# Small counting steps placed between the steps of a sort, a product moved from VectorE to ScalarE, and an activation table loaded early

The chip is one Trainium2; the kernel runs on one of its cores. The metric is device time in microseconds (us) of one launch, lower is better.

## The reference

A graph attention layer: 4096 nodes with 64 features, 50000 edges, 4 heads of 64 outputs, all in fp32. Loops over heads are written short here.

```python
x_proj[h] = x @ weight[h]
score[h, e] = sum(x_proj[h, src[e]] * att_src[h]) + sum(x_proj[h, dst[e]] * att_dst[h])
score = where(score > 0, score, 0.2 * score)
output[h, dst[e]] += exp(score[h, e]) * x_proj[h, src[e]]
total[h, dst[e]]  += exp(score[h, e])
return (output / (total + 1e-8)).transpose(1, 0, 2).reshape(4096, 256)
```

The edges come in random order. The kernel sorts them twice on VectorE, so that all edges of a block of destinations lie together, and then works block by block.

## The kernel before

The edges lie as 128 rows of 391. A first sort orders each row and merges rows in runs of eight. It is a chain of compare steps, each a pair of VectorE instructions (a minimum and a maximum) that read one buffer and write the next. The sorted rows are stored to memory, and for each group of nodes the right stretch of every run is fetched back. Where a stretch starts follows from counting how many sources lie below a bound. That takes three engines: ScalarE forms a Sign against each of sixteen bounds and adds it up (`below`), TensorE adds the rows of a run (`counts`), and VectorE turns that into addresses (`bounds`).

```python
def runs(self, to=None, fine=0, between=()):
    ...
    for m in range(1, 3):                      # the second and third round of merging rows
        self.turn()                            # transpose
        self.opposed(m)
        for j in range(m - 1, -1, -1):
            self.half(j)
        self.turn()
        last = fine if m == 2 else 0
        todo = list(between) if m == 2 else []
        for j in range(8, last - 1, -1):
            self.half(j, to=to if m == 2 and j == last else None)
            if todo:
                todo.pop(0)(self.a[self.cur])  # one small step behind each pair
...
def bounds(pool, cps, nt, n, off, mask, nk, ws, we):
    for i, ps in enumerate(cps):               # two counts, seven small instructions each
        cnt = pool.tile([P, nt + 1], F32, name=f"cnt{i}")
        V.tensor_scalar(out=cnt[:], in0=ps[:], scalar1=-0.5, scalar2=RUN * n / 2, ...)
        for o, t in ((0, ws), (1, we)):
            ...                                # pick, reduce, add the offset
...
def fetch(pool, skey, start, n, to, what):
    if start.dtype == I32:
        wi = start
    else:
        wi = pool.tile([P, w], I32, name=f"wi{what}")[:]
        V.tensor_copy(out=wi, in_=start)       # the addresses as integers
    for i in range(w):
        G.indirect_dma_start(out=to[:, i * n:(i + 1) * n], in_=skey[:, :], in_offset=..., ...)
...
sgn = below(so1, av(eS[:], 0, [2, EL]), EL, nb1, NR, NR)
for e, n in ((0, EH), (EH, EL - EH)):          # the sort keys, in two halves
    V.tensor_scalar(out=sli[:, c], in0=src, scalar1=SG - 1, ..., op0=OP.bitwise_and)
    V.tensor_scalar(out=tF[:, c], in0=sli[:, c], scalar1=1.0 - N, ..., op0=OP.mult)
    V.scalar_tensor_tensor(out=uF[:, c], in0=dst, scalar=float(SG), in1=tF[:, c], ...)
    V.scalar_tensor_tensor(out=key[:, c], in0=src, scalar=float(N), in1=uF[:, c], ...)
tables(pr, pps, pp1)                           # attention tables: TensorE and ScalarE
so.rows(1, EL)
cps = counts(so1, pp1, sgn, NR, [sel1[:, 0, :], sel1[:, 1, :]])
store(skey1, so.runs())
bounds(so1, cps, NR, EL, off1, m16, NR, ws1, we1)
...
stretches = group(so2, Lent(), ws1[:], (relative, split))   # fetch, then the second sort
```

In the traces each engine takes its instructions in the order of the program. `tables` stands ahead of `counts`, and both use TensorE.

## Time and profile before

| | us |
|---|---|
| median of 3 runs (range) | 292.44 (291.14 to 292.70) |
| span of the profiled run | 291.7 |
| VectorE / TensorE / ScalarE busy | 262.4 / 202.9 / 185.7 |
| first step of the first sort | 6.88 |
| counts on TensorE | 62.66 |
| sorted rows stored, stretches fetched | 68.18, 72.39 |
| first step of the second sort | 76.55 |

The prediction below shows the seam between the sorts and the lines around it. What it only refers to is the start. These are lines of the timeline of the kernel before; the columns are start in us, busy us, engine, line of the source, operation, output and inputs with shapes, number of instructions, and in brackets the idle time in front with what ended it.

```profile
4.38 0.26 DVE L697 TENSOR_SCALAR tF<-sli 128x195 f32<-128x195 int32 x1
4.68 0.36 DVE L698 SCALAR_TENSOR_TENSOR uF<-eD,tF 128x195 f32<-128x195 int32 x1
...
5.48 1.28 ACT L279 ACT_TABLE_LOAD   x1 [5.48 <-DVE key L699]
...
6.77 0.65 ACT L279 ACTIVATE junk<-eS,nb 128x391 f32<-128x391 int32 x1
6.88 0.36 DVE L200 TENSOR_TENSOR sA<-key 128x196 f32<-128x196 f32 x1
```

The key is made on VectorE, line by line. ScalarE loads its table (1.28 us) only at 5.48, because in the program as built the load carries the first Sign's waits for the edges; the bracket names VectorE, which ended at the same moment.

### The profile page before, as it was taken

The numbers are of one execution on the slowest core, as the hardware profiler recorded it, in microseconds if no ns is written. First come the engines' busy times: TensorE is split into PE (matmuls) and PEld (weight loads), VectorE is DVE, ScalarE is ACT, GpSimd is POOL, SyncE is SP. The second block draws the span as 40 slices with busy tenths as digits, with TensorE's granted clock in tenths as the row PEclk, the third lists the DMA queues.
The fourth block names the chain that finished last, engine by engine and source line by source line (L and its number), as shares of the span: only waits on it lengthen the run. The fifth ranks groups of instructions, "written<-read, shape, count | busy, mean of one in ns | idle before, by whom it ended". The sixth has DMA issues, their size and how long they took to land.

```text
span 291.7 us, 8543 instructions
## 1 busy us (share of the span) xinstructions
PE 202.9 (70%) x3546; PEld 194.6 (67%) x3546; DVE 262.4 (90%) x536; ACT 185.7 (64%) x360; POOL 27.6 (9%) x78
## 2 busy tenths in 40 slices
PE   0001899970000027478999999999999999999990
PEld 0000599970000015268999999999999999999980
DVE  5999999996499999698999999999999999999970
ACT  2960710031499946484787878888888878787850
POOL 7882000000200000600000000000000000000000
PEclk9999975555555558887999999999999999999998
DMA  3026000001100001186776767767586757675011
GB/s 110 0 50 115 0 2 0 0 1 37 36 0 0 0 0 39 50 322 212 274 292 218 280 234 256 252 237 285 204 286 229 287 199 299 234 265 183 22 37 42
DMA packets 13327, 40.75 MB, mean 140 GB/s; under 512 B 3121, under 2 KB 8913, under 8 KB 9313
## 3 DMA queue, kind: packets, MB, share of 16 engines
q1 hardware_dynamic: 10768, 37.91, 36.2%
q10 hardware_dynamic: 1808, 1.56, 2.4%
q0 software_dynamic: 704, 0.66, 0.9%
q8 instruction: 30, 0.49, 0.7%
q14 instruction: 17, 0.13, 0.1%
HBM read 35.08 MB, written 5.05 MB: 138 GB/s over the span
## 4 chain that ended last, share of the span: by engine, by line

## 5 line engine op out<-in xcount | busy, mean ns | idle before, releaser
L531 ACT CAST xs<-ps 128x1200 bf16<-128x1200 f32 (+1 forms) x99 | 103.9, 1049 | 0.0
L549 DVE TENSOR_TENSOR val<-xs,wv 128x4096 bf16<-128x4096 bf16 (+1 forms) x34 | 75.4, 2221 | 0.4 <-ACT xs L531 0.2
L523 PE MATMUL ps<-adb,oh 128*128 128x136 bf16 x528 | 62.1, 224 | 0.0
L574 PE MATMUL acc<-xs,val 128*128 128x125 bf16 x1024 | 61.8, 218 | 0.0
L521 PE MATMUL ps<-xa,oh 128*128 128x72 bf16 x528 | 59.4, 197 | 3.4 <-DVE oh L500 2.2
L574 PEld LDWEIGHTS <-val 128*128 128x128 bf16 x1056 | 58.8, 98 | 0.0
L523 PEld LDWEIGHTS <-oh 128*128 128x128 bf16 x528 | 49.5, 99 | 1.3 <-issue 1.2
L521 PEld LDWEIGHTS <-oh 128*128 128x128 bf16 x528 | 47.3, 99 | 2.7 <-DVE oh L500 2.7
L529 ACT ACTIVATE ex<-ps 128x96 bf16<-128x96 f32 (+1 forms) x99 | 25.0, 252 | 31.7 <-PE ps L527 29.5
L500 DVE TENSOR_SCALAR oh<-bc,pF 128x4096 bf16<-128x4096 bf16 (+2 forms) x37 | 42.5, 1148 | 1.2 <-ACT bc L487 1.2
L211 DVE TENSOR_TENSOR sA<-sB 128x256 f32<-128x256 f32 (+2 forms) x104 | 37.3, 399 | 1.7
L211 DVE TENSOR_TENSOR sB<-sA 128x256 f32<-128x256 f32 (+2 forms) x98 | 35.1, 399 | 1.6
L527 PE MATMUL ps<-xa,oh 128*128 128x72 bf16 x528 | 33.5, 198 | 0.0
L290 PE MATMUL cnt_ps<-sgn,sel 128*128 128x17 f32 (+1 forms) x6 | 1.7, 390 | 42.0 <-ACT sgn L282 42.0
L290 PEld LDWEIGHTS cnt_ps<-sgn,sel 128*128 128x128 f32 x6 | 1.4, 317 | 42.1 <-issue 42.1
L527 PEld LDWEIGHTS <-oh 128*128 128x128 bf16 x528 | 26.5, 99 | 0.0
L503 DVE TENSOR_SCALAR oh<-bc,pF 128x2048 bf16<-128x2048 bf16 (+2 forms) x37 | 25.5, 690 | 0.0
L424 PEld LDWEIGHTS at_ps<-uv,xT 64*128 64x128 f32 x130 | 25.2, 301 | 0.2 <-issue 0.2
L424 PE MATMUL at_ps<-uv,xT 64*128 64x4 f32 x130 | 25.3, 331 | 0.0
L279 ACT ACTIVATE junk<-kr,nb 128x512 f32<-128x512 f32 x33 | 23.8, 722 | 1.1
L631 PE MATMUL pf<-Wbd,aT 128*128 128x128 f32 x132 | 23.1, 298 | 0.8 <-ACT aT L626 0.8
L407 PE MATMUL ps<-ident,wS 64*128 64x64 f32 x2 | 0.7, 350 | 28.0 <-DMA wS<-in_weight_dram 28.0
(144 smaller groups left out, 238.5 us busy)
## 6 DMA issues: line engine op xcount, KB each, us to landing
bc<-gat_bins SPq DMA_DIRECT2D x31, 1024.0 KB
out_dram<-res SPq DMA_DIRECT2D x32, 125.0 KB
eD<-in_edge_index_dram ACTq DMA_DIRECT2D x2, 195.0 KB
eS<-in_edge_index_dram SPq DMA_DIRECT2D x2, 195.0 KB
gat_bins<-tb SPq DMA_DIRECT2D x10, 32.0 KB
gat_sorted<-sA SPq DMA_DIRECT2D x1, 256.0 KB
gat_sorted<-ki SPq DMA_DIRECT2D x1, 256.0 KB
win<-gat_sorted,to POOLq DMA_INDIRECT x5, 2.9
```

The source lines that it names most:

```text
L211: V.tensor_tensor(out=av(d[:], o, [2 * h, n], [1, h]), in0=av(s[:], 0, [2 * h, n], [1, h]), in1=av(s[:], h, [2 * h, n], [1, h]), op=op)
L279: S.activation(out=junk[:], in_=v, func=ACTF.Sign, bias=nbnd[:, b:b + 1], scale=1.0, accum_out=sgn[:, b:b + 1])
L424: T.matmul(out=ps[:, b, :], lhsT=xT[:, b * step:b * step + P], rhs=uv[:, k, :], start=(b == 0), stop=True, skip_group_check=True)
L500: V.tensor_scalar(out=oh[:, 0:2, e], in0=bc[:, :, e], scalar1=pF[:, 0:1], scalar2=None, op0=OP.is_equal)
L503: V.tensor_scalar(out=oh[:, 2, e], in0=bc[:, 1, e], scalar1=pF[:, 1:2], scalar2=None, op0=OP.is_equal)
L521: T.matmul(out=ps[:, i, P:P + XC], lhsT=oh[:, 1, e], rhs=xa[:, 2 * t, :], start=(i % 2 == 0), stop=False, skip_group_check=True)
L523: T.matmul(out=ps[:, i, 0:S0], lhsT=oh[:, 0, e], rhs=adb[:, b, :], start=False, stop=False, skip_group_check=True)
L527: T.matmul(out=ps[:, i, P:P + XC], lhsT=oh[:, 2, t * W2:(t + 1) * W2], rhs=xa[:, 2 * t + 1, :], start=False, stop=True, skip_group_check=True)
L529: S.activation(out=av(ex[:], 2 * t0, [2, n], [2 * NT, 2 * H], [1, 2]), in_=av(ps[:], P, [PW, n], [1, 2 * H], [0, 2]), func=ACTF.Exp)
L531: S.copy(out=xs[:, t0:t0 + n, 0:P + XC], in_=ps[:, 0:n, 0:P + XC])
L549: V.tensor_tensor(out=av(val[:], h * Dout, [Dout, n], [C, NT], [1, Din]), in0=av(xs[:], S0, [0, n], [XW, NT], [1, Din]), in1=av(wv[:], h * ...
L574: T.matmul(out=self.to[k], lhsT=val[:, t, k * P:(k + 1) * P], rhs=xs[:, t, 0:BD], start=apart and t == 0, stop=(t == NT - 1), skip_group_c ...
```

## The change

Three intentions. The fourteen small steps of `bounds` and the cast of the addresses go between the compare steps of the first sort (nine in the second of the three rounds of merging, six in the third), so that the fetch need not wait for them. One of the four key instructions per half goes to ScalarE. ScalarE's table is loaded while it has nothing to do, and the Signs follow the key.

```diff
+    first = cst.tile([1, 2], F32)
+    V.memset(first[:], 0.0)
+    S.activation(out=first[:, 0:1], in_=first[:, 1:2], func=ACTF.Sign)
...
+    wi1 = cst.tile([P, 2], I32)
...
-        def runs(self, to=None, fine=0, between=()):
+        def runs(self, to=None, fine=0, between=(), ahead=()):
...
-                todo = list(between) if m == 2 else []
+                todo = list(between if m == 2 else ahead)
...
-    def bounds(pool, cps, nt, n, off, mask, nk, ws, we):
+    def bounds(pool, cps, nt, n, off, mask, nk, ws, we, wi):
         (the same instructions, gathered in a list "steps")
+        steps.append(lambda: V.tensor_copy(out=wi[:], in_=ws[:]))
+        return [lambda keys, f=f: f() for f in steps]
...
-        sgn = below(so1, av(eS[:], 0, [2, EL]), EL, nb1, NR, NR)
...
-            V.tensor_scalar(out=tF[:, c], in0=sli[:, c], scalar1=1.0 - N, scalar2=None, op0=OP.mult)
-            V.scalar_tensor_tensor(out=uF[:, c], in0=dst, scalar=float(SG), in1=tF[:, c], op0=OP.mult, op1=OP.add)
+            S.mul(out=tF[:, c], in_=dst, mul=float(SG))
+            V.scalar_tensor_tensor(out=uF[:, c], in0=sli[:, c], scalar=1.0 - N, in1=tF[:, c], op0=OP.mult, op1=OP.add)
...
+        sgn = below(so1, av(eS[:], 0, [2, EL]), EL, nb1, NR, NR)
         tables(pr, pps, pp1)
         so.rows(1, EL)
         cps = counts(so1, pp1, sgn, NR, [sel1[:, 0, :], sel1[:, 1, :]])
-        store(skey1, so.runs())
-        bounds(so1, cps, NR, EL, off1, m16, NR, ws1, we1)
+        steps = bounds(so1, cps, NR, EL, off1, m16, NR, ws1, we1, wi1)
+        store(skey1, so.runs(ahead=steps[:9], between=steps[9:]))
...
-        stretches = group(so2, Lent(), ws1[:], (relative, split))
+        stretches = group(so2, Lent(), wi1[:], (relative, split))
```

More of the change, by code (lines that the diff above doesn't have):

```diff
@@ L292, in counts @@
         return cps
-    def bounds(pool, cps, nt, n, off, mask, nk, ws, we):
+    def bounds(pool, cps, nt, n, off, mask, nk, ws, we, wi):
+        steps = []
         ni = ws.shape[1] // len(cps)
         for i, ps in enumerate(cps):
+            c = slice(i * ni, (i + 1) * ni)
             cnt = pool.tile([P, nt + 1], F32, name=f"cnt{i}")
-            V.tensor_scalar(out=cnt[:], in0=ps[:], scalar1=-0.5, scalar2=RUN * n / 2, op0=OP.mult, op1=OP.add)
+            steps.append(lambda cnt=cnt, ps=ps: V.tensor_scalar(
+                out=cnt[:], in0=ps[:], scalar1=-0.5, scalar2=RUN * n / 2, op0=OP.mult, op1=OP.add))
             for o, t in ((0, ws), (1, we)):
                 pick = pool.tile([P, ni, nk], F32, name=f"pick{i}{o}")
-                V.tensor_tensor(out=pick[:], in0=av(cnt[:], o, [nk, ni], [1, nk]),
-                                in1=av(mask[:], 0, [0, ni], [1, nk]), op=OP.mult)
-                V.tensor_reduce(out=t[:, i * ni:(i + 1) * ni], in_=pick[:], axis=AX, op=OP.add)
-                V.tensor_tensor(out=t[:, i * ni:(i + 1) * ni], in0=t[:, i * ni:(i + 1) * ni],
-                                in1=av(off[:], i, [0, ni]), op=OP.add)
+                steps += [
+                    lambda cnt=cnt, pick=pick, o=o: V.tensor_tensor(
+                        out=pick[:], in0=av(cnt[:], o, [nk, ni], [1, nk]), in1=av(mask[:], 0, [0, ni], [1, nk]),
+                        op=OP.mult),
+                    lambda pick=pick, c=c, t=t: V.tensor_reduce(out=t[:, c], in_=pick[:], axis=AX, op=OP.add),
+                    lambda c=c, t=t, i=i: V.tensor_tensor(out=t[:, c], in0=t[:, c], in1=av(off[:], i, [0, ni]),
+                                                          op=OP.add)]
+        steps.append(lambda: V.tensor_copy(out=wi[:], in_=ws[:]))
+        return [lambda keys, f=f: f() for f in steps]
     class Stretches:
```

## The prediction

> **What bounds the kernel now.** I read the page's busy slices first, then the timeline of the start, of the first sort and of the seam behind it, then the timeline of the second sort, where the kernel already does what the change wants for the first. Slices are 7.29 us each (291.7 us / 40).
>
> ```profile
> PE   0001899970000027478999999999999999999990
> DVE  5999999996499999698999999999999999999970
> ```
>
> VectorE works without a break through both sorts except in slices 9 and 10 (65.6 to 80.2 us): the seam between the first sort and the second. Nothing else is to be had before 107 us, so a microsecond lost or won on VectorE up to there moves the end by the same amount: the second sort and the blocks that follow start from the fetch at the seam. The seam, in the timeline:
>
> ```profile
> 68.07 0.17 DVE L299 TENSOR_SCALAR cnt<-cnt_ps 128x17 f32<-128x17 f32 x1
> 68.18 0.34 SPq L271 DMA_DIRECT2D gat_sorted<-sA  x1
> ...
> 71.38 0.17 DVE L362 CAST wi<-ws 128x2 int32<-128x2 f32 x1 [0.43 <-issue]
> 72.39 1.07 POOL L364 DMA_INDIRECT raw<-gat_sorted,wi  x1 [48.38 <-DVE wi L362]
> ...
> 76.55 0.42 DVE L200 TENSOR_TENSOR sA<-raw 128x256 f32<-128x256 f32 x1 [5.00 <-DMA raw<-gat_sorted,wi]
> ```
>
> The sorted rows are stored at 68.18. Then fourteen small VectorE instructions (L299 to L305, two counts) and the cast L362 run alone, and the fetch starts only at 72.39, 4.21 us after the store was issued. This is what the change aims at. What it overlooks, or does not, stands in the same timeline, on TensorE:
>
> ```profile
> 37.46 22.70 PE L424 MATMUL at_ps<-uv,xT 64*128 64x4 f32 x118
> ...
> 49.99 0.76 DVE L211 TENSOR_TENSOR sA<-sB 128x256 f32<-128x256 f32 x2
> 50.78 0.76 DVE L211 TENSOR_TENSOR sB<-sA 128x256 f32<-128x256 f32 x2
> ...
> 59.81 2.91 PE L424 MATMUL at_ps<-uv,xT 64*128 64x4 f32 x13
> ...
> 62.66 1.03 PE L290 MATMUL cnt_ps<-sgn,sel 128*128 128x17 f32 x4
> ```
>
> The products L290, which add the signs into the counts, stand in TensorE's order behind the attention tables (L424), and run only at 62.66. Their signs were complete long before: the last of the sixteen Sign instructions starts at 18.42. In the kernel before this delay is free, because L299 reads the counts at 68.07.
>
> **What the Trainium skill says.** (1) "TensorE: Matmul & The Clock Gate", Part 1, on engine queue depths, and Part 3, "What overlaps and what doesn't": VectorE and ScalarE are strict first-in-first-out, and matmuls start and end in program order. The trace agrees: L290 waits some 43 us with its input ready. (2) "VectorE: DVE Perf Modes", "The DRAIN you can't avoid": the next instruction does not start until the pipe is empty, and a semaphore costs nothing extra. The trace agrees only in part: L320 (next fence) starts at 108.11, before the pair beside it has ended (108.20). (3) "DMA: Bandwidth & Descriptors", "Anatomy of one DMA": a transfer's fixed cost, about 2.0 us in the page's fit for the GpSimd path, is mostly the receipt of the write, heaviest for HBM. This store is on SyncE's queue, but the trace has its like: the second store is issued at 113.39 and the fetch that needs it starts at 116.12, 2.73 us. (4) "ScalarE: Activation LUTs", "What ACT_TABLE_LOAD costs": about 1283 ns for the load. The trace agrees with 1.28 us.
>
> **The change part by part.**
>
> *Small steps between sorting steps.* The second sort shows their price:
>
> ```profile
> 107.44 0.76 DVE L211 TENSOR_TENSOR sA<-sB 128x256 f32<-128x256 f32 x2
> 108.11 0.20 DVE L320 TENSOR_SCALAR cnt<-cnt_ps 128x41 f32<-128x41 f32 x1
> 108.23 0.76 DVE L211 TENSOR_TENSOR sB<-sA 128x256 f32<-128x256 f32 x2
> ...
> 110.72 0.19 DVE L325 TENSOR_TENSOR pick<-cnt,m 128x40 f32<-128x40 f32 x1
> 110.83 0.76 DVE L211 TENSOR_TENSOR sA<-sB 128x256 f32<-128x256 f32 x2
> 111.51 0.19 DVE L327 TENSOR_REDUCE sum<-pick 128x5 f32<-128x40 f32 x1
> 111.63 0.76 DVE L211 TENSOR_TENSOR sB<-sA 128x256 f32<-128x256 f32 x2
> ```
>
> With a small step behind it a pair takes 0.79, 0.80 and 0.81 us (108.23 - 107.44 and so on); without one, as from 49.99 to 50.78, it takes 0.79. The step fits into the pair's tail. Fifteen at about 0.01 us make +0.15 us.
>
> *The seam.* With the fetch's addresses ready before the sort ends, the fetch waits for the store alone: 2.73 us by the second store's example, perhaps 0.1 more for the longer list of semaphores. 4.21 - 2.8 = -1.4 us.
>
> *The front.* Before, the key is four VectorE instructions per half. L697 goes to ScalarE, and its share is the step from one start to the next, 4.68 - 4.38 = 0.30 us, so 0.6 us at most for two halves. It will be less: VectorE now waits for ScalarE's product, which waits for the destinations to land. The table load in the kernel before waits for all sources and starts at 5.48, so I take 5.4 as the landing of the second halves. A ScalarE product of 195 elements is an estimate of 0.4 to 0.5 us (a Sign of 391 took 0.65; the page in (4) gives 0.833 ns for each of the 196 elements less, and 93 ns for the bias pointer that a product lacks). The second product then ends near 5.9, and the sort starts some 0.25 us earlier than 6.88.
>
> *The table load.* It moves to the idle start, so the first Sign starts at about 5.9 and not at 6.77: -0.9 us on ScalarE. ScalarE issues the loads of x and of the weights after its Signs, and TensorE's first product waits for those, at 28.04. So TensorE's whole row moves by -0.9, the counts too.
>
> *The new wait.* Here I leave the intent of the change. In the changed program as built, the first step (the count's scaling, with a wait on TensorE) stands on VectorE directly behind the first pair that follows the second transposition, which is the pair at 49.99 in the kernel before; nine of the fifteen steps are placed in this earlier round. TensorE's order is as before: tables, then counts. The first count needs two of L290's four passes: 62.66 + 1.03/2 = 63.2, less 0.9 gives 62.3. VectorE reaches the step at 50.75 - 0.25 = 50.5 and stands still until 62.3, about 11.8 us. The pair that started at 50.78 then starts near 62.4: +11.6 us. The 0.25 us won at the front lies inside this wait and is worth nothing; the 0.9 us on ScalarE is counted, as it ends the wait earlier.
>
> The sum for the fetch: +11.6 (wait, front and table load included) + 0.15 (steps) - 1.4 (seam) = +10.35 us. From the fetch on, every instruction is the same and hangs on the fetched rows, so I carry +10.35 to the end: 292.44 + 10.35 = 302.8 us.
>
> **The rivals.** *A. The wait does not bite,* and the seam's gain arrives whole: -1.4 - 0.25 + 0.15, about 291.0 us. It would need the counts on TensorE by 50.5 us. For it speaks only that the signs are ready near 19; against it, that the order is built into the program and that TensorE is busy without a gap from 37.46 on. *B. TensorE's end moves far more than ScalarE's 0.9 us.* The granted clock is 1.00 until about 40.4 and 0.50 from then to 63. The products come every 0.10 us before that and every 0.20 after, so every microsecond for which the full clock lasts longer brings the end a microsecond forward. If the drop stays at its time while the tables start 0.9 us earlier, the wait ends near 61.4 and the time is 301.9. If the clock is at half from the start of TensorE's work, which no view of this run suggests, the tables end several microseconds later: 305 to 308. *C. The seam gains nothing* because the store lands later than its like: the fetch then waits as long as before, and the time is 304.2. *D. Later work swallows the delay.* The tables of TensorE and the loads of x are done in time in either kernel, and the blocks wait for the sorted rows; I see no slack there.
>
> **Range and chances.** The wait's beginning is known to some 0.3 us, its end to about 1.5 us (landing of the loads, the clock), the seam to 0.5 us, the spread of runs to 0.8 us (291.14 to 292.7). Together some 2.4 us to each side: 300.3 to 305.2. Slower by over 2% begins at 298.3, 4.5 us below the prediction, so 0.94 for slower. 0.04 for within 2% if the wait is half as long, 0.02 for faster.
>
> **What would show it.** The changed profile should show: VectorE with a hole of 10.5 to 12.5 us near 50.5, ended by TensorE, in front of the count's scaling; the counts' products near 61.8 right behind the tables; ScalarE's table load in the first 4 us and the first Sign near 5.9; pairs of 0.80 us with small steps between them; store to fetch in 2.6 to 3.1 us; from the fetched rows to the end the same length as now (291.7 - 72.4 = 219.3 us). I am wrong in the main point if VectorE passes the first step without waiting, and wrong in size if the products L424 end clearly off 61.8.

## The result, and the profile after

| | before | changed |
|---|---|---|
| median of 4 runs, us | 292.57 | 303.55 |
| range, us | 291.14 to 293.18 | 302.15 to 304.81 |
| span of the profiled run, us | 291.7 | 301.8 |

The ratio is 1.0381, with a 95% interval of 1.0322 to 1.0441: slower. Ratios here are the mean time of one kernel's fast runs over that of the other's of the same rounds, so not quite the ratio of the medians quoted. All outputs are right.

These are the busy tenths of the changed kernel in forty slices, now of 7.55 us each.

```profile
PE   0003999930000002765999999999999999999990
DVE  5999996079549999997899999999999999999970
```

VectorE has a new hole: the digits 6, 0, 7 stand for 45 to 68 us, where VectorE was busy throughout before. The timeline of the changed kernel there:

```profile
49.85 0.76 DVE L216 TENSOR_TENSOR sA<-sB 128x256 f32<-128x256 f32 x2
...
61.61 1.03 PE L295 MATMUL cnt_ps<-sgn,sel 128*128 128x17 f32 x4
...
62.26 0.18 DVE L306 TENSOR_SCALAR cnt<-cnt_ps 128x17 f32<-128x17 f32 x1 [11.65 <-PE cnt_ps L295]
62.35 0.75 DVE L216 TENSOR_TENSOR sB<-sA 128x256 f32<-128x256 f32 x2
63.02 0.17 DVE L311 TENSOR_TENSOR pick<-cnt,m 128x16 f32<-128x16 f32 x1
63.14 0.76 DVE L216 TENSOR_TENSOR sA<-sB 128x256 f32<-128x256 f32 x2
```

The bracket on L306 carries the result: VectorE stood still for 11.65 us in front of the count's scaling, and TensorE's counts ended that. The counts ran at 61.61, as late as ever. The pair at 62.35 is the one that ran at 50.78 before: +11.57 us. Behind it pairs follow every 0.79 us, small steps and all. The seam of the changed kernel:

```profile
77.24 0.16 DVE L317 CAST wi<-ws 128x2 int32<-128x2 f32 x1
...
79.74 0.34 SPq L276 DMA_DIRECT2D gat_sorted<-sA  x1
82.77 1.06 POOL L376 DMA_INDIRECT raw<-gat_sorted,wi  x1 [55.58 <-issue]
...
87.16 0.72 ACT L384 ACTIVATE kr<-raw,goff 128x512 f32<-128x512 f32 x1 [21.39 <-DMA raw<-gat_sorted,wi]
87.31 0.43 DVE L205 TENSOR_TENSOR sA<-raw 128x256 f32<-128x256 f32 x1 [7.60 <-DMA raw<-gat_sorted,wi]
```

The addresses are ready before the rows are stored, and the fetch follows the store by 3.03 us (82.77 - 79.74) where it took 4.21. That part of the intent works. From there to the first step of the second sort, though, it takes 4.54 us (87.31 - 82.77) and took 4.16 (76.55 - 72.39), so a third of what was won is lost again. And the start of the changed kernel:

```profile
2.17 1.28 ACT L85 ACT_TABLE_LOAD   x1 [2.17 <-DVE pm_i L98]
...
5.55 0.38 ACT L708 ACTIVATE tF<-eD 128x196 f32<-128x196 int32 x1 [1.11 <-DMA eD<-in_edge_index_dram]
...
5.83 0.63 ACT L284 ACTIVATE junk<-eS,nb 128x391 f32<-128x391 int32 x1
5.96 0.36 DVE L709 SCALAR_TENSOR_TENSOR uF<-sli,tF 128x196 f32<-128x196 int32 x1 [0.32 <-ACT tF L708]
...
6.75 0.36 DVE L205 TENSOR_TENSOR sA<-key 128x196 f32<-128x196 f32 x1
```

The table is loaded at 2.17 and the first Sign starts 0.94 us earlier. The sort starts only 0.13 us earlier, since VectorE now waits for ScalarE, which waited for the edges.

### The profile page after: what moved, and what is told of

Same layout as the page of the kernel before. It is cut to its first block, busy times and chain, and to the rows that moved or that the text cites. A ratio compares the mean times of both kernels' runs of the same rounds, so it can differ in the third digit from the quotient of the medians.

```text
span 301.8 us, 8547 instructions
## 1 busy us (share of the span) xinstructions
PE 201.5 (67%) x3546; PEld 193.5 (64%) x3546; DVE 260.4 (86%) x535; ACT 186.5 (62%) x363; POOL 28.8 (10%) x78
## 3 DMA queue, kind: packets, MB, share of 16 engines
q1 hardware_dynamic: 10768, 37.91, 34.6%
## 4 chain that ended last, share of the span: by engine, by line
```

## The experiments

My theory after the result: the loss is the wait for TensorE, whose counts stand behind the tables in its order; the small steps themselves are free. Rivals: the broken-up second round or the steps cost the time; the moved front matters. There is a second question, where the seam's gain comes from and why a part is lost behind the fetch. The kernel before ran at 292.87 to 292.91.

### Counts ahead of the tables

```diff
+        cps = counts(so1, pp1, sgn, NR, [sel1[:, 0, :], sel1[:, 1, :]])
         tables(pr, pps, pp1)
         so.rows(1, EL)
-        cps = counts(so1, pp1, sgn, NR, [sel1[:, 0, :], sel1[:, 1, :]])
```

> The changed kernel with one edit: the two products that form the counts stand on TensorE ahead of the tables instead of behind them. My theory (VectorE stands behind TensorE's tables): the hole near 50 us vanishes, VectorE runs on through the first sort, the seam keeps its gain (4.2 us before, 3.0 after); the time is that of the kernel before less about 1.2 us (seam) and 0.15 us (front) plus 0.15 us (small steps): about 291.3 us, ratio to before 0.996. Rival (the small steps themselves, or the second round being broken up, slow the sort): the time stays near 303.

Measured: 292.17 us (6 runs, 290.60 to 293.14), ratio 0.9961 (0.9920 to 1.0002). From the timeline of this kernel:

```profile
50.03 0.76 DVE L216 TENSOR_TENSOR sA<-sB 128x256 f32<-128x256 f32 x2
50.70 0.17 DVE L306 TENSOR_SCALAR cnt<-cnt_ps 128x17 f32<-128x17 f32 x1
50.82 0.76 DVE L216 TENSOR_TENSOR sB<-sA 128x256 f32<-128x256 f32 x2
```

The hole is gone with this one edit, and with it the whole loss; the same steps stand in the same places. The counts now run at 18.57. The rival falls. The ratio is as expected, but its interval just touches 1, so the gain over the kernel before is read from the seam (3.04 us from store to fetch), not shown by the time.

### The same without the new front

The edit above, and the front undone in the changed kernel:

```diff
-    first = cst.tile([1, 2], F32)
-    V.memset(first[:], 0.0)
-    S.activation(out=first[:, 0:1], in_=first[:, 1:2], func=ACTF.Sign)
...
+        sgn = below(so1, av(eS[:], 0, [2, EL]), EL, nb1, NR, NR)
         for e, n in ((0, EH), (EH, EL - EH)):
...
-            S.mul(out=tF[:, c], in_=dst, mul=float(SG))
-            V.scalar_tensor_tensor(out=uF[:, c], in0=sli[:, c], scalar=1.0 - N, in1=tF[:, c], ...)
+            V.tensor_scalar(out=tF[:, c], in0=sli[:, c], scalar1=1.0 - N, scalar2=None, op0=OP.mult)
+            V.scalar_tensor_tensor(out=uF[:, c], in0=dst, scalar=float(SG), in1=tF[:, c], ...)
...
-        sgn = below(so1, av(eS[:], 0, [2, EL]), EL, nb1, NR, NR)
```

> As e1_counts_first, but with the key and the table load as in the kernel before: only the small steps and the early counts. Theory: the seam's gain alone, about 291.4 us; it differs from e1_counts_first by the front's 0.15 us, not resolved in the time, but readable as the start of the sort (6.88 against 6.75). Rival (the front carries the gain): as slow as the kernel before, 292.6.

Measured: 292.50 us, ratio 0.9958 (0.9919 to 0.9997), store to fetch 3.05 us. The sort starts at 6.91, and in the kernel above, with the front, at 6.94. A kernel further down that lacks the front started at 6.70. So what the front is worth on VectorE does not stand out of the scatter of that start, and the rival, that it carries the gain, falls.

### The front alone

The kernel before with the diff just shown turned round: `first`, `S.mul`, and `below` behind the key.

> The kernel before with the changed front alone (early table load, destinations scaled on ScalarE). Theory: the sort starts 0.13 us earlier, so the time is 292.4, same as before. Rival (the front is worth the two VectorE instructions it removes, 0.6 us): 292.0.

Measured: 292.87 us, ratio 1.0005 (0.9970 to 1.0039), sort started at 6.69. As the theory says: nothing. A gain of 0.2% (the rival's) would still lie inside the interval, but the start read from the trace is 0.19 us early, not 0.6. The seam of this kernel is that of the kernel before, and store to fetch took 4.04 us here (71.98 - 67.94) against 4.21: a scatter to keep in mind below.

### The changed kernel without the front

The changed kernel with that same diff, counts behind the tables.

> The changed kernel with the front undone, the small steps kept, the counts behind the tables. Theory: the wait ends with TensorE, which starts about 1.0 us later without the early table load: about 304.5 us, hole ended at 63.2. Rival (front irrelevant to the wait): 303.5.

Measured: 303.64 us, ratio 1.0374 (1.0329 to 1.0418), the hole 10.90 us long and ended at 61.63. My expectation missed. ScalarE did issue the loads of x at 18.47 and not at 17.56, but in the profiled run the weights landed sooner: TensorE's first product started at 26.42, against 27.06 in the changed kernel with its earlier issue. From the issue of x to that product the profiled runs took 9.6 us (before), 9.5 (changed), 8.6 (front alone) and 8.0 (this one). The landing thus scatters by more than the 0.94 us that the front moves the issue, and the time does not resolve what the front is worth there.

### Sixteen more products in front of the counts

```diff
+        more = pps.tile([P, 16, H], F32, tag="pp")
+        for b in range(16):
+            T.matmul(out=more[:, b, :], lhsT=ident[0:64, :], rhs=ident[0:64, 0:H], start=(b == 0), stop=True, ...)
         cps = counts(so1, pp1, sgn, NR, [sel1[:, 0, :], sel1[:, 1, :]])
```

> The changed kernel with sixteen more products of the tables' shape on TensorE between the tables and the counts (their results go nowhere). At the half clock the tables' products came every 0.197 us, two records each: 16 x 2 x 0.197 = 6.3 us. Theory: the hole on VectorE grows by 6.3 us and the time to about 309.8. Rival (VectorE waits for something else): no change, 303.5.

In the changed kernel: 310.76 us, ratio 1.0613 (1.0569 to 1.0657), 7.2 us above the changed kernel's median.

```profile
70.03 0.18 DVE L306 TENSOR_SCALAR cnt<-cnt_ps 128x17 f32<-128x17 f32 x1 [19.28 <-PE cnt_ps L295]
```

The hole grew by 7.63 us (19.28 - 11.65), as TensorE's counts came 7.77 us later (69.38 against 61.61). Of that the sixteen products took 6.89 us (69.38 - 62.49, where they start), 0.43 us each and not 0.39. The other 0.88 us is the tables' later end (62.49 against 61.61): TensorE's first product came 0.30 us later, and its granted clock (the share of full speed that the throttle leaves it) fell to half near 39.0 us and not near 40.5. The end of the hole moved by the same 7.77 us (70.03 against 62.26): the coupling is one to one.

> The kernel before with the same sixteen products at the same place. Theory: its counts are then formed at 69.0 us and the first scaling, which came at 68.1, waits for them: about 1 to 1.5 us of the 6.3 show, 293.8 us, so the kernel before had some 4.9 us of room there. Rival (no room, TensorE on the path): 298.9.

In the kernel before: 294.68 us, ratio 1.0043 (0.9989 to 1.0097).

```profile
70.52 0.18 DVE L299 TENSOR_SCALAR cnt<-cnt_ps 128x17 f32<-128x17 f32 x1 [2.42 <-PE cnt_ps L290]
```

Its counts came at 69.87 instead of 62.66, 7.2 us later (the products took 6.89 us here too, 69.87 - 62.98), and of that 2.42 us show as a wait; the rest went into the room that the kernel before has there. In the time the 1.8 us between the medians are not resolved. The same edit costs all in one kernel and a third in the other: this is what "off the path" meant for the counts before the change, and what the change gave up.

### All steps in the last round

```diff
-        store(skey1, so.runs(ahead=steps[:9], between=steps[9:]))
+        both = [lambda keys, p=steps[i:i + 2]: [f(keys) for f in p] for i in range(0, len(steps), 2)]
+        store(skey1, so.runs(between=both))
```

> The changed kernel with all fifteen small steps in the last round, two behind each of eight sorting steps, counts still behind the tables. Theory: VectorE reaches the first step near 61.6 and the counts are there at 62.2, so the hole shrinks from 11.7 to about 0.6 us; two dependent steps in one place no longer fit the tail, some 0.2 us each time, 1.4 in all; seam gain 1.2: about 293.2 us, same as before. Rival (the wait is always about 12 us long): 303.

Measured: 293.80 us, ratio 1.0031 (0.9993 to 1.0069).

```profile
62.30 0.18 DVE L306 TENSOR_SCALAR cnt<-cnt_ps 128x17 f32<-128x17 f32 x1 [0.58 <-PE cnt_ps L295]
```

The wait is 0.58 us, ended at the same time as in the changed kernel (62.30 against 62.26). So, with the counts at the same time, the wait is as long as VectorE is early. The store is issued at 69.69, 1.5 us later than before, of which 0.58 is the wait and the rest the pairs of dependent steps.

### Control: the kernel before with early counts

The edit of the first experiment, in the kernel before.

> The kernel before with only the counts moved ahead of the tables on TensorE. Control. Theory: TensorE was not on the path, the time stays at 292.6. Rival (the early counts are worth something by themselves): faster than 292.

Measured: 291.81 us, ratio 0.9948 (0.9905 to 0.9991). I had expected no change, and this is a small gain. The trace shows where a part of it lies: store to fetch took 3.66 us and not 4.21, store to first step 7.94 and not 8.37. The addresses were as late as before (cast at 71.44 against 71.38), but the fetch followed the end of the cast by 0.28 us where it had taken 0.84. In the program as built, the fetch of the kernel before waits for nine semaphores (the counters by which an engine or a transfer says that it is done), TensorE's after VectorE's as the last; here it waits for eight, with VectorE's last. Whether the number or the order makes the difference, this run does not show. This opened the second question.

### VectorE takes its waits early

```diff
+        so = Sorter(pool, raw)
+        V.memset(so.a[1][:, 0:1], 0.0)
         kr = pool.tile([P, L], F32, name="kr")
         ...
-        so = Sorter(pool, raw)
```

> e1_counts_first plus a one-column VectorE memset on the sort's next buffer, placed while the store is in flight, so that the fourteen semaphores of that recycled memory are waited for there and not by the first step of the second sort. In the earlier runs the first step began 8.37 us after the store was issued in the kernel before and 7.51 in e1_counts_first, where the fetch itself had moved by 1.17 (4.21 to 3.04): 0.31 was lost behind the fetch. My theory (the list of semaphores, which the removed cast had taken): the lost 0.3 us comes back, store to first step 7.2 us. Rival (the fetch itself takes longer when it starts earlier): no change, 7.5.

Measured: 291.54 us, ratio 0.9940 (0.9902 to 0.9978). From the timeline of this kernel:

```profile
70.53 0.06 DVE L384 MEMSET sA<- 128x1 f32 x1 [2.38 <-DMA gat_sorted<-sA]
...
75.46 0.43 DVE L205 TENSOR_TENSOR sA<-raw 128x256 f32<-128x256 f32 x1 [4.87 <-DMA raw<-gat_sorted,wi]
75.59 0.72 ACT L386 ACTIVATE kr<-raw,goff 128x512 f32<-128x512 f32 x1 [8.93 <-DMA raw<-gat_sorted,wi]
```

Store to first step took 7.29 us (75.46 - 68.17), against 7.51 in the first experiment, where the fetch left at the same distance (3.04 and 3.05). VectorE starts ahead of ScalarE again, as in the kernel before; in the changed kernel it starts 0.15 us behind it. As built, VectorE's first step in the changed kernel waits for fourteen semaphores, because it writes memory that the first sort had used, and here for three. In the kernel before the cast had taken these waits, since its output lay in such memory; moving the cast left them to the first instruction behind the fetched data. Most of the expected 0.3 us came back.

### The fetched rows in memory of their own

```diff
+    raw1 = cst.tile([P, L], F32)
...
-        raw = pool.tile([P, L], F32, name="raw")
+        raw = (raw1 if between else pool.tile([P, L], F32, name="raw"))
...
+        S.copy(out=kr[:, 0:1], in_=goff[:, 0:1])
```

> As e9_vector_waits_early, and the fetched rows have memory of their own, so that the fetch waits for three semaphores instead of ten; ScalarE takes its waits early too. Theory: store to fetch 2.7 us as for the second store (3.04 in e1_counts_first), store to first step about 6.9; time about 291.3 us, some 0.6 under e1_counts_first. Rival (the landing of the store alone sets the fetch at 3.04): no change.

Measured: 291.31 us (289.95 to 292.23), ratio 0.9926 (0.9890 to 0.9962): the lowest median, though not resolved from the section before, 0.7% faster than the kernel before of the same rounds, and 12 us below the changed kernel's median. Its fetch waits for three semaphores, not ten, and left 2.87 us behind the store (71.04 - 68.17); the first step came 7.17 us behind it. The direction is the theory's, the size is less: 0.17 us at the fetch where I had expected 0.34. The long list's distance is 3.03 to 3.05 in seven profiled runs, so 0.17 stands clear of the scatter.

```profile
68.17 0.34 SPq L277 DMA_DIRECT2D gat_sorted<-sA  x1
70.35 0.19 ACT L387 COPY kr<-goff 128x1 f32<-128x1 f32 x1 [3.68 <-DMA gat_sorted<-sA]
70.53 0.06 DVE L385 MEMSET sA<- 128x1 f32 x1 [2.38 <-DMA gat_sorted<-sA]
71.04 1.06 POOL L377 DMA_INDIRECT raw<-gat_sorted,wi  x1 [43.96 <-DVE sA L385]
```

In the program as built, all three instructions below the store wait for its landing. ScalarE's copy starts 2.18 us behind the store, the fetch 2.87 us. So the store had landed by 70.35, and the remaining 0.69 us in front of the fetch is not the landing: the rival falls. What GpSimd spends it on is not shown.

### Only the cast in memory of its own

```diff
+    wi1 = cst.tile([P, 2], I32)
...
         bounds(so1, cps, NR, EL, off1, m16, NR, ws1, we1)
+        V.tensor_copy(out=wi1[:], in_=ws1[:])
...
-        stretches = group(so2, Lent(), ws1[:], (relative, split))
+        stretches = group(so2, Lent(), wi1[:], (relative, split))
```

> The kernel before with one edit: the cast of the addresses writes memory of its own instead of memory that the sort had used; all fifteen small steps stay behind the sort, counts behind the tables. In the kernel before the cast waits for the landing of the store (its memory is recycled) and the fetch waits for the cast. Theory: most of the seam's gain does not come from moving the steps but from this: store to fetch about 3.3 us (4.21 before, 3.03 in the changed kernel), time about 292.2. Rival (the fourteen steps set the seam): store to fetch stays above 3.9.

Measured: 292.53 us, ratio 0.9991 (0.9958 to 1.0024), store to fetch 3.85 us. This theory fell in its strong form: freeing the cast alone brings 0.36 of the 1.18 us, and only 0.19 against the 4.04 of the front-alone kernel. The cast did come earlier (70.81 against 71.38), but then the fetch followed its end by 1.01 us, with five semaphores listed behind VectorE's. And the first step of the second sort came 8.40 us behind the store, as late as in the kernel before (8.37): what the cast no longer waited for, the first step waited for.

### All three memory edits, steps left behind the sort

The diff just shown, and the edits of the two sections before it:

```diff
+        so = Sorter(pool, raw)
+        V.memset(so.a[1][:, 0:1], 0.0)
         kr = pool.tile([P, L], F32, name="kr")
+        S.copy(out=kr[:, 0:1], in_=goff[:, 0:1])
...
-        raw = pool.tile([P, L], F32, name="raw")
+        raw = (raw1 if between else pool.tile([P, L], F32, name="raw"))
```

> e11_cast_in_own_memory with the other two edits of e10_own_memory; the small steps stay behind the sort. Theory: the addresses are ready 2.97 us after the store (fourteen steps and the cast), the fetch follows at about 3.2, store to first step about 7.3; so what the moved steps are worth, against e10_own_memory, is 0.4 to 0.5 us. Rival (the steps are worth their whole 2.9 us): more than 1 us behind e10_own_memory.

Measured: 291.86 us, ratio 0.9957 (0.9918 to 0.9996). Store to fetch took 3.31 us, the fetch followed the cast's end by 0.46 (three semaphores), and store to first step took 7.60. That is the changed kernel's seam (7.57) without moving one step. Against the kernel with the same edits and the steps inside the sort (7.17), moving them is worth 0.43 us, as expected; the times, 291.86 and 291.31, do not resolve that. The two kernels also differ in the front and in the place of the counts, so the 0.43 us is not cleanly the steps'.

## Why the prediction was right

The time, 303.55, lies in the range of 300.3 to 305.2, 0.75 us above the predicted 302.8. The range's 2.4 us to each side is a judgement: its four terms add up to 3.1, or to 1.8 as independent ones. By its steps:

- **The new wait** was the main step, and it holds. Predicted: a hole of 11.8 us from 50.5 to 62.3; measured 11.65 us, ended at 62.26. That TensorE's order causes it is shown by three interventions: counts ahead of the tables remove it, a longer row of products lengthens it one to one, steps in the last round shrink it to 0.58 us.
- **Small steps.** Predicted 0.15 us for fifteen; measured none. From the pair behind the first step to the store the kernel before took 17.40 us (68.18 - 50.78), the changed one with fourteen steps inside 17.39 (79.74 - 62.35).
- **The seam** was mis-sized. Predicted -1.4 us at the fetch; measured -1.18 (4.21 - 3.03), and only -0.80 at the first step of the second sort (8.37 - 7.57). The example I took, the second store, has a fetch with two semaphores to wait for; I allowed 0.1 us for the longer list, and the fetch came 0.2 us later than that; a list of three semaphores brought 0.17 us back. The size of the gain hangs on one run of the kernel before: against the 4.04 of the front-alone kernel it is 1.01. That VectorE would inherit the cast's waits behind the fetch I did not see; taking them early brought back 0.22 us.
- **The front.** Predicted -0.25 us for the sort's start, measured -0.13 (inside the scatter of that start, 6.69 to 6.96 over the runs), and worth nothing, as I said, since it falls in front of the wait. The estimate for ScalarE's product was 0.4 to 0.5 us; it took 0.38. **The table load:** predicted -0.9 us for the Signs, measured -0.94, and -0.98 at TensorE's first product. That last agreement is partly luck: without the front the wait ended 0.6 us earlier still, because the landing of the weights scatters.
- **From the fetch on**: predicted unchanged at 219.3 us, measured 219.0 (301.8 - 82.77). At the fetch the terms give +11.57 - 0.01 - 1.18 = +10.38 us, against +10.35 predicted; the spans differ by 10.1, the medians by 11.0. The 0.38 us lost behind the fetch does not show in the 219.0, so that agreement is no finer than the scatter of the spans (300.3 to 303.0 in the four runs).
- **The rivals.** A and D are refuted by the hole and by the unchanged rest. C, a seam without gain, did not happen. Of B, a drop of TensorE's clock at a fixed time is not what the traces show: with the first product at 28.04, 27.06 and 26.11 (before, changed, front alone) the granted clock fell to half near 40.4, 40.5 and 38.4, that is 12.4, 13.4 and 12.3 us into TensorE's work. Over all fourteen profiled runs it fell 10.8 to 13.9 us in, so this too scatters, and with it the end of the wait: where it fell 11.5 us in (only the cast in memory of its own), the counts came 35.3 us behind the first product (61.66 - 26.32), against 34.6 in the changed kernel.

What stays open: what sets the scatter in the landing of the weights, what sets the moment at which TensorE's clock falls, and how each semaphore in a list is paid for. The longest lists go with the longest gaps here, but eight semaphores went with a shorter gap than three (0.28 and 0.46 us), and no run changed the fetch's list and nothing else.

## What to carry to other kernels

Before moving work into the gaps of a busy engine, ask when its inputs are produced, and in which engine's queue that product stands: an input that was late without harm becomes a wait in the middle of the path. If the producer's own inputs are early, move the producer first; here one line of order took away a loss of 3.8%. And when an instruction is taken out of a seam, look at what it had waited for on behalf of the next one, above all where memory is reused.

## What the Trainium skill lacked or had wrong

- "TensorE: Matmul & The Clock Gate", Part 1, calls the half clock the idle state and the full clock the busy one. Here the granted clock was 1.00 through the first 27 us, in which TensorE did nothing, and fell to 0.50 near 40.5 us amid unbroken products of four output columns; it stayed there for the remaining 21 us of them. The products came every 0.10 us before the fall and every 0.20 us after it, as the recorded clock says; for the idle stretch there is the record alone.
- "VectorE: DVE Perf Modes", "The DRAIN you can't avoid", says that the next instruction does not start until the pipe is empty, then that one that is not held starts earlier; it gives no number for what fits in. Here fourteen small instructions that do not depend on the pair in front of them cost nothing measurable between the pairs of the sort (17.39 against 17.40 us).
- None of the pages drawn on here says what a list of semaphores costs in front of an instruction. A fetch followed the end of its last input by 1.01 us with eleven semaphores in its list, by 0.84 with nine, by 0.28 with eight and by 0.46 with three, where in both the last input's stood at the end.
- None of them says how far the landing of the same loads scatters: from the issue of x to the first product that needs the weights it took 7.8 to 10.2 us over the fourteen profiled runs.
